# Moving the last two loads of a streaming gradient kernel ahead of a store in the DMA queue

## The chip, the cores and the metric

One core of a Trainium2 chip. The metric is the device time of one execution in microseconds; several executions are timed and the median is given. A profile of one execution has a slightly shorter span than its time (1245.0 us of 1247.06 us in the first profile), so times are compared with times and spans with spans.

## The reference

```python
# x: (8192, 8192) float32
def reference(x):
    return np.gradient(x, axis=1)
```

Inside a row the result is half the difference of the right and the left neighbour; at the two ends it is the plain difference of the last two elements. 268.4 MB are read and 268.4 MB written.

## The kernel before

The rows are cut into 32 sets of 256 rows. A set is 128 partitions with two rows each, 64 KB a partition, 8 MB in all. Three buffers hold three sets. A set is loaded 64 elements to the right of the start of its buffer, and VectorE writes the result over it in place. GpSimd first saves the end differences. Loads and stores all go through one queue, which issues them in program order and waits at each for what it needs: in the profile L30 is issued at 1128.24 us and L31, the next, at 1147.54, S28 having landed at 1147.53.

```python
slots = [pool.tile([P, SH + W], f32, ...) for k in range(NB)]     # NB = 3, SH = 64, W = 2 * 8192

def load(i):                                # waits for the store that frees the buffer
    b = slots[i % NB]
    ins = nc.sync.dma_start(out=b[:, SH : SH + W], in_=x_sets[i])
    loads.append(chain(i, ins, *([stores[i - NB]] if i >= NB else [])))

for i in range(NB):
    load(i)
for i in range(nsets):                      # nsets = 32
    ...                                     # GpSimd: ends of the rows
    last = i == nsets - 1
    nr = 1 if last else R                   # the last set goes in two halves
    for r in range(0, R, nr):
        ins = nc.vector._custom_dve(...)    # half the difference of the neighbours, in place
        ...                                 # VectorE or GpSimd: put the ends in
        ins = nc.sync.dma_start(out=out_sets[i, :, ...], in_=b[:, ...])
        stores[i] = chain(i, ins, placed)
    if i % NB == NB - 1:                    # after each third store: the next three loads
        for k in range(i + 1, min(i + 1 + NB, nsets)):
            load(k)
```

(Cuts are marked with "...".) So the queue holds three loads, three stores, three loads and so on. In what follows L0 to L31 are loads and S0 to S31 stores. The last entries are L27 L28 L29, S27 S28 S29, L30 L31, S30, S31a, S31b. A "turn" is the place where the queue goes over from loads to stores or back.

Of the kernel before, what the change touches and what calls it, by code (L numbers as in the profile page):

```python
# [1 line left out]

# [4 lines left out]


@with_exitstack
def kernel(  # L10
    ctx: ExitStack,
    tc: tile.TileContext,
    x: bass.AP,
    out: bass.AP,
):










    nc = tc.nc
    P = nc.NUM_PARTITIONS  # L27
    n, m = x.shape  # L28
    R = 2  # L29
    NB = 3  # L30
    SH = 64  # L31
    W = R * m
    nsets = n // (P * R)
    f32 = x.dtype

    x_sets = x.rearrange("(s p t) m -> s p (t m)", p=P, t=R)
    out_sets = out.rearrange("(s p t) m -> s p (t m)", p=P, t=R)

    pool = ctx.enter_context(tc.tile_pool(name="pool", bufs=1))
    slots = [pool.tile([P, SH + W], f32, name=f"slot{k}", tag=f"slot{k}") for k in range(NB)]  # L40
    ends = pool.tile([P, nsets, R, 2], f32, name="ends", tag="ends")
    loads, stores = [], [None] * nsets
    in_front = {}

    def chain(i, ins, *needed):



        group, engine = f"slot{i % NB}", ins.ins.engine
        keep = [o.ins for o in needed]  # L50
        if in_front.get(engine, (None,))[0] == group:
            keep.append(in_front[engine][1])
        tc.declare_no_dep(ins.ins, group=group, keep=keep, reason="implied by the needed step")
        tc.add_to_no_dep_group(group, ins.ins)
        in_front[engine] = group, ins.ins
        return ins

    def load(i):
        b = slots[i % NB]
        ins = nc.sync.dma_start(out=b[:, SH : SH + W], in_=x_sets[i])  # L60
        loads.append(chain(i, ins, *([stores[i - NB]] if i >= NB else [])))

    with tc.manual_schedule():
        for i in range(NB):
            load(i)
        for i in range(nsets):
            b = slots[i % NB]
            xin = b[:, SH : SH + W].rearrange("p (t m) -> p t m", m=m)

            ins = nc.gpsimd.tensor_sub(  # L70
                out=ends[:, i, :, :],
                in0=xin[:, :, 1 : m : m - 2],
                in1=xin[:, :, 0 : m - 1 : m - 2],
            )
            at = [chain(i, ins, loads[i])]
            last = i == nsets - 1
            nr = 1 if last else R
            for r in range(0, R, nr):
                c0, c1 = r * m + 1, (r + nr) * m - 1

                ins = nc.vector._custom_dve(  # L81
                    dve_ops.TENSOR_TENSOR_REDUCE_SUB_MAX,
                    out=b[:, c0:c1],
                    in0=b[:, SH + c0 + 1 : SH + c1 + 1],
                    in1=b[:, SH + c0 - 1 : SH + c1 - 1],
                    s0=0.0,
                    s1=0.5,
                )
                halved = chain(i, ins, *at)
                res = b[:, r * m : (r + nr) * m].rearrange("p (t m) -> p t m", m=m)  # L90
                placer = nc.gpsimd if i % 5 in (1, 3) and not last else nc.vector
                ins = placer.tensor_copy(out=res[:, :, 0 : m : m - 1], in_=ends[:, i, r : r + nr, :])  # L92
                placed = chain(i, ins, halved)
                ins = nc.sync.dma_start(
                    out=out_sets[i, :, r * m : (r + nr) * m], in_=b[:, r * m : (r + nr) * m]
                )
                stores[i] = chain(i, ins, placed)
                at = [halved]
            if i % NB == NB - 1:
                for k in range(i + 1, min(i + 1 + NB, nsets)):  # L100
                    load(k)


# [1 line left out]
_INS = ['x']  # L105
_OUTS = [((8192, 8192), 'float32')]


# [23 lines left out]
```

## Time and profile before

| | |
|---|---|
| time, 3 executions | 1247.18 us median (1247.16 to 1247.86) |
| span of the profile | 1245.0 us |
| DMA, share of 16 engines | 99.8% |
| VectorE busy | 45% |
| waits of the queue for stores (before loads) | 373.2 us in total |

Two views matter here. The stretches give, for a stretch of time, its length, the busy time of VectorE and GpSimd, the clock, the DMA share and the GB/s; a DMA packet is counted where it starts. In the order of time each row has a start, a duration, the engine and the operation, and in brackets how long the engine was idle before and what ended that. GpSimd's small subtraction (TENSOR_TENSOR) is the first thing that happens to a set after its load has wholly landed, so its start marks the landing on the slowest of the 16 DMA engines: in the packet records (see the experiments) the engines of the kernel before end L31 from 1202.48 to 1205.05 us, and GpSimd starts on it at 1205.53. These two rows of the kernel before, in the order of time, will be compared with all later runs; they are the landings of L30 and L31:

```profile
1186.19 0.20 POOL L70 TENSOR_TENSOR ends<-slot 128x4 f32<-128x4 f32 x1 [77.05 <-DMA slot<-in_x_dram]
1205.53 0.20 POOL L70 TENSOR_TENSOR ends<-slot 128x4 f32<-128x4 f32 x1 [19.14 <-DMA slot<-in_x_dram]
```

They are 19.34 us apart, eight packets of 2.418 us: the slowest engine lost nothing on L31. The bracket of the second row (19.14 us of idle time) says the same; a larger figure there is lost time.

### The profile page before, as it was taken

The numbers are of one execution on the slowest core, as the hardware profiler recorded it, in microseconds if no ns is written. First come the engines' busy times: TensorE is split into PE (matmuls) and PEld (weight loads), VectorE is DVE, ScalarE is ACT, GpSimd is POOL, SyncE is SP. The second block draws the span as 40 slices with busy tenths as digits, with TensorE's granted clock in tenths as the row PEclk, the third lists the DMA queues.
The fourth block names the chain that finished last, engine by engine and source line by source line (L and its number), as shares of the span: only waits on it lengthen the run. The fifth ranks groups of instructions, "written<-read, shape, count | busy, mean of one in ns | idle before, by whom it ended". The sixth has DMA issues, their size and how long they took to land.

```text
span 1245.0 us, 241 instructions
## 1 busy us (share of the span) xinstructions
DVE 554.8 (45%) x54; POOL 8.8 (1%) x48
## 2 busy tenths in 40 slices
DVE  2850483079009603850582079009603840591083
POOL 0000000000000000000000000000000000000000
DMA  9999999999999999999999999999999999999999
GB/s 404 438 436 419 425 438 438 438 438 438 434 427 421 436 438 438 436 438 432 432 419 438 436 438 432 436 434 432 423 436 436 436 438 436 430 427 430 436 411 404
DMA packets 9361, 536.88 MB, mean 431 GB/s; under 512 B 1040, under 2 KB 1040, under 8 KB 1040
## 3 DMA queue, kind: packets, MB, share of 16 engines
q1 hardware_dynamic: 9360, 536.88, 99.8%
q14 instruction: 1, 0.01, 0.0%
HBM read 268.44 MB, written 268.44 MB: 431 GB/s over the span
## 4 chain that ended last, share of the span: by engine, by line
another core or an unknown queue 74%; DVE 18%; DMA 3%; issue 2%; POOL 1%; SPq 0%; POOLq 0%
DVE slot L81 18%; DMA slot<-in_x_dram 3%; POOL ends L70 0%; POOL slot L92 0%; SPq L60 0%; DVE slot L92 0%; POOLq L127 0%
## 5 line engine op out<-in xcount | busy, mean ns | idle before, releaser
L81 DVE CUSTOM_DVE_ANT_0 slot<-slot 128x16382 f32<-128x16382 f32 (+1 forms) x33 | 551.3, 16706 | 667.9 <-POOL ends L70 667.9
L70 POOL TENSOR_TENSOR ends<-slot 128x4 f32<-128x4 f32 x32 | 6.3, 198 | 988.8 <-DMA slot<-in_x_dram 988.8
L92 DVE COPY slot<-ends 128x4 f32<-128x4 f32 (+1 forms) x21 | 3.6, 172 | 0.7
L92 POOL COPY slot<-ends 128x4 f32<-128x4 f32 x12 | 2.3, 190 | 207.9 <-DVE slot L81 207.9
L116 POOL MEMSET const-bfloat16-1.0<- 128x1 bf16 x1 | 0.1, 102 | 0.0
L116 POOL MEMSET const-uint8-127<- 128x1 uint8 x1 | 0.1, 102 | 0.0
L116 POOL MEMSET const-float32-0.0<- 128x1 f32 x1 | 0.1, 99 | 0.2 <-issue 0.2
L116 POOL MEMSET const-float32-1.0<- 128x1 f32 x1 | 0.1, 99 | 0.0
## 6 DMA issues: line engine op xcount, KB each, us to landing
out_dram<-slot SPq DMA_DIRECT2D x2, 4096.0 KB, 20.2
slot<-in_x_dram SPq DMA_DIRECT2D x32, 58.0
out_dram<-slot SPq DMA_DIRECT2D x31, 40.3
```

The costliest lines, as they stand in the source:

```text
L70: ins = nc.gpsimd.tensor_sub(out=ends[:, i, :, :], in0=xin[:, :, 1 : m : m - 2], in1=xin[:, :, 0 : m - 1 : m - 2],)
L81: ins = nc.vector._custom_dve(dve_ops.TENSOR_TENSOR_REDUCE_SUB_MAX, out=b[:, c0:c1], in0=b[:, SH + c0 + 1 : SH + c1 + 1], in1=b[:, SH + c0 ...
L92: ins = placer.tensor_copy(out=res[:, :, 0 : m : m - 1], in_=ends[:, i, r : r + nr, :])
L116: nc = _bacc.Bacc("TRN2", target_bir_lowering=False, num_devices=1)
```

## The change

The intent is to have the last two loads in early, since the end of the kernel is load, compute, store with nothing left to overlap, and since S29 is ready long ahead of S30 (issued at 1126.63 and 1203.88 us in the profile of before) and can fill the engines later. L30 and L31 are issued after S28 instead of after S29.

```diff
+    n3 = (nsets - 2) // NB * NB
+    assert nsets - 2 == n3
+    next_loads = {i: range(i + 1, i + 1 + NB) for i in range(NB - 1, n3 - NB, NB)}
+    next_loads[n3 - 2] = range(n3, nsets)
 ...
-            if i % NB == NB - 1:
-                for k in range(i + 1, min(i + 1 + NB, nsets)):
+            if i in next_loads:
+                for k in next_loads[i]:
                     load(k)
```

## The prediction

> **What bounds the kernel now.** I read the page first, then the waits of the queue that issues the DMAs, then the order of the last issues in time, and last the DMA share in narrow stretches at the end.
>
> The page shows that nothing but DMA is near its limit:
>
> ```profile
> span 1245.0 us, 241 instructions
> ...
> DVE 554.8 (45%) x54; POOL 8.8 (1%) x48
> ...
> DMA  9999999999999999999999999999999999999999
> GB/s 404 438 436 419 425 438 438 438 438 438 434 427 421 436 438 438 436 438 432 432 419 438 436 438 432 436 434 432 423 436 436 436 438 436 430 427 430 436 411 404
> ...
> q1 hardware_dynamic: 9360, 536.88, 99.8%
> ```
>
> VectorE works 45% of the span; the 16 DMA engines are at 9 tenths in every slice and 99.8% busy on the one queue in use. 536.88 MB is the input read once plus the output written once, so the bytes cannot shrink. The best slices run at 438 GB/s; 536.88 MB at 435 GB/s would be 1234 us, 11 us (0.9%) less than the span. That is more than any reordering can win, and the start and the end have their part in it.
>
> Names: L0 to L31 are the 8 MB loads, S0 to S31 the stores (S31 in two halves, a and b). One 8 MB transfer takes 8.389 MB / 435 GB/s = 19.3 us. The queue's own waits:
>
> ```profile
> SPq L94 <- DVE slot L92: 525.7, 21, 55.9
> SPq L60 <- DMA out_dram<-slot: 373.2, 29, 19.2
> SPq L94 <- POOL slot L92: 298.8, 12, 36.7
> ```
>
> The issuing queue waits nearly always, but for things behind which data is still queued: a load waits for a store two transfers back, while one more is in the engines. Waiting there costs nothing unless the engines run dry. So I looked for a place where they do. The last group in order of time:
>
> ```profile
> 1109.17 17.22 DVE L81 CUSTOM_DVE_ANT_0 slot<-slot 128x16382 f32<-128x16382 f32 x1 [2.13 <-POOL ends L70]
> ...
> 1126.63 0.33 SPq L94 DMA_DIRECT2D out_dram<-slot  x1
> 1128.24 19.64 SPq L60 DMA_DIRECT2D slot<-in_x_dram  x2
> ...
> 1186.42 17.23 DVE L81 CUSTOM_DVE_ANT_0 slot<-slot 128x16382 f32<-128x16382 f32 x1 [59.81 <-POOL ends L70]
> ...
> 1203.88 19.93 SPq L94 DMA_DIRECT2D out_dram<-slot  x3
> ...
> 1205.76 8.69 DVE L81 CUSTOM_DVE_ANT_0 slot<-slot 128x8190 f32<-128x8190 f32 x1 [1.91 <-POOL ends L70]
> ```
>
> S29 is issued at 1126.63, L30 at 1128.24, L31 19.3 us later (1147.54 when that row is looked at alone), then nothing until S30 at 1203.88. S30 can't be issued before VectorE is through with L30's data. L31 is the only transfer between L30's landing and S30, so there the engines can run dry, and narrow stretches show that they do (share and GB/s count a packet where it starts; a packet is 64 KB on one engine and takes 2.4 us, so 16 starts in 0.5 us read 2097 GB/s):
>
> ```profile
> 1166.60:1185.90 19.30, 0.00 (x0) 0.00 (x0) 1.00 1.00 435
> 1185.90:1205.20 19.30, 17.40 (x2) 0.20 (x1) 1.00 0.95 411
> ...
> 1199.80:1200.30 0.50, 0.50 (x1) 0.00 (x0) 1.00 2.72 1180
> 1200.30:1202.20 1.90, 1.90 (x1) 0.00 (x0) 1.00 0.56 241
> 1202.20:1202.70 0.50, 0.50 (x1) 0.00 (x0) 1.00 0.91 393
> 1202.70:1204.70 2.00, 1.11 (x2) 0.00 (x0) 1.00 0.00 0
> 1204.70:1205.20 0.50, 0.00 (x0) 0.00 (x0) 1.00 4.91 2097
> ```
>
> The last packets of L31 start spread over 1199.8 to 1202.7: nine in the first half microsecond (1180 GB/s x 0.5 us / 65.5 KB), seven in the next 1.9 us, then three, on late engines that also started one in the first half microsecond (the 16 engines, three of them twice, are the 19). Nobody starts anything in the next 2.0 us, and all 16 start S30 together at 1204.7 to 1205.2. So there is a hole, 0 to 2.4 us depending on the engine; from the packet records the mean is 1.6 us. But the engines that began last, at 1202.2 to 1202.7, are done 2.4 us later, at 1204.6 to 1205.1: for the slowest engine the hole is about nothing. In the packet records its L31 share ends at 1205.05, and its S30, S31a and S31b shares end 19.32, 9.68 and 9.68 us later, at 1243.73, where the data ends. It never waits.
>
> [...]
>
> **The change part by part.** Removed and added: nothing; 67 instructions on the issuing queue in both, the same on the other engines. The order of instructions shows one move: S28, S29, L30, L31, S30 becomes S28, L30, L31, S29, S30. Each 8 MB transfer is a slot of 19.3 us in the engines; they change places.
>
> 1. L30 waits for S27 as before (1128.2), L31 for S28 as before (1147.5). These issue times don't move. S29, ready at 1126.6, is issued behind L31: about 1147.9, 21 us later.
> 2. While L31 is held, the engines have the rest of S28 (to 1147.3) and L30 (to 1166.6). L31 and S29 are there from 1147.9, 19 us before L30 ends. No hole opens.
> 3. Data slots after: L30 1147.3 to 1166.6, L31 1166.6 to 1185.9, S29 1185.9 to 1205.2, S30 1205.2 to 1224.5, S31 1224.5 to 1243.8. L30 and L31 come 19.3 us earlier, S29 38.6 us later, S30 and S31 stay.
> 4. VectorE on L30: about 1167.1 to 1184.3; S30 issued about 1184.6, some 20 us before its slot. On L31: halves at 1186.4 and 1195.1; S31a issued about 1195.3, S31b 1204.1, 29 and 30 us before their slots. The hole closes: 1.6 us of mean engine idleness goes.
> 5. On the path that sets the end: the slowest engine's own chain of packets. It had about 0.0 us of hole, so it gets back 0.0 us. The leading engines end up to 2.4 us earlier and then have nothing to do. Sum: 1247.18 - 0.0; I take 0.1 us off for S30's start, which then lies behind queued data for every engine. Prediction 1247.1 us.
>
> **The rivals.** (a) The hole is paid back in full. If the 16 engines shared one limit, idle engines would be lost capacity and the end would come 1.6 us earlier: 1245.6 us. Against it: packets take 2.418 us with all 16 busy, and those of the engines that ran alone during the hole take 2.42 to 2.45; no engine goes faster when others are idle. The lag is also each engine's own history: the spread of the finishing times grows from 0.48 us after five transfers to 2.57 us at L31, and nothing lets the late ones catch up. (b) The final compute is exposed. If VectorE's 17.4 us after L31's landing lay bare at the end, moving L31 forward by 19.3 us would win up to that: about 1230 us. Against it: S30's 19.3 us cover the first half (8.7 us, S31a issued at 1214.7 for a slot at 1224.5) and S31a's 9.7 us the second (issued 1223.47, 11 us before its slot). (c) The queue stalls in a new place. If L31's wait for S28 held S29 while the engines ran out, it would cost; with L30's 19.3 us queued ahead and about 1 us from issue to the first packet, there are 18 us of margin. [...] (d) Chance: the lag of the slowest engine comes from scattered slow packets (up to 1 us of excess) and differs from run to run; the three runs spread over 0.7 us.
>
> **Range and chances.** The centre is 1247.1. Below, rival (a) in full gives 1245.6; above, a new small wait or an unlucky set of slow packets gives a microsecond. 1245.5 to 1248.3 should hold it 8 times in 10. Two per cent is 25 us, which no rival but (b) comes near, and that not wholly: faster 0.01, same 0.985, slower 0.005.
>
> **What would show it right or wrong.** Right: L30 and L31 land 39 us after issue in place of 57.9; S29 is issued near 1147.9; the queue's last stores are issued near 1184.6, 1195.3 and 1204.1; the stretch 1185.9 to 1205.2 reads a share of 1.00; VectorE is through by 1204 and not 1223; the data still ends at about 1243.7 and the span stays at 1245. The engines should end spread out by some 2.5 us, not together within 0.2 us. Wrong: all engines end together a microsecond or two earlier (rival a), or a stretch of low DMA share appears between 1147 and 1186 (rival c), or the slow packets bunch in another place.

Its sum came to 1247.18 - 0.0 - 0.1 = 1247.1 us (the 0.1 us is the author's estimate, with no trace behind it).

## The result

| | median | range | executions |
|---|---|---|---|
| before, same job | 1247.59 us | 1247.16 to 1248.12 | 6 |
| changed | 1248.45 us | 1248.12 to 1249.27 | 6 |

The ratio is 1.0008, with a 95% interval of 0.9995 to 1.002: the same, within 2%. Ratios are the mean time of one kernel's fast runs over that of the other's of the same rounds, so not quite the ratio of the medians. The changed kernel is 1.35 us over the predicted 1247.1 us and 0.15 us over the upper end of the range. No gain was forecast and none came; what has to be explained is the microsecond in the other direction.

The page of the changed kernel, where it answers to that of before:

```profile
span 1246.3 us, 241 instructions
...
DVE 554.8 (45%) x54; POOL 8.8 (1%) x48
...
GB/s 404 438 438 433 419 427 438 438 438 438 433 433 429 423 435 438 435 438 431 433 433 433 427 435 431 438 438 435 433 433 438 421 431 438 438 435 433 435 431 358
```

VectorE has done the same work in the same time. The last slice but one moved 431 GB/s where it had moved 411, the last one 358 where it had moved 404: the transfers are packed closer ahead of the end and thin out in it.

The end in order of time (rows between are left out):

```profile
1148.46 57.32 SPq L103 DMA_DIRECT2D out_dram<-slot  x4
1167.45 0.20 POOL L79 TENSOR_TENSOR ends<-slot 128x4 f32<-128x4 f32 x1 [57.76 <-DMA slot<-in_x_dram]
...
1187.50 0.20 POOL L79 TENSOR_TENSOR ends<-slot 128x4 f32<-128x4 f32 x1 [19.85 <-DMA slot<-in_x_dram]
...
1205.25 0.17 DVE L101 COPY slot<-ends 128x2 f32<-128x2 f32 x1
```

S29 is issued at 1148.46, L30 has landed at 1167.45 and VectorE is through at 1205.42, all as forecast. But L31 lands at 1187.50, 20.05 us after L30 and not 19.34: the slowest engine lost 0.71 us there that it did not lose before (0.73 in the packet records, whose step was 20.05 against 19.32).

The stretches of the changed kernel:

```profile
1185.90:1205.20 19.30, 17.43 (x3) 0.20 (x1) 1.00 1.00 435
1202.70:1204.70 2.00, 2.00 (x1) 0.00 (x0) 1.00 0.61 262
...
1239.70:1240.70 1.00, 0.00 (x0) 0.00 (x0) 1.00 1.06 459
1240.70:1243.20 2.50, 0.00 (x0) 0.00 (x0) 1.00 0.34 144
1243.20:1243.90 0.70, 0.00 (x0) 0.00 (x0) 1.00 0.22 94
```

The hole is closed: the share over 1185.9 to 1205.2 is 1.00, and packets go on starting between 1202.7 and 1204.7, where none did before. At the very end the packets are 32 KB. In the first row of the end 14 of them start in 1.0 us (459 GB/s x 1.0 us / 32.8 KB), about the full rate of 435 GB/s; in the next 2.5 us only 11 (full rate would be 33), in the last 0.7 us two. Some engines are done while others still work. In the packet records the first engine ends at 1240.98 and the last at 1245.07, 4.09 us apart; in the kernel before all ended between 1243.57 and 1243.73.

Between these two profiles the data ends 1.34 us later (1245.07 against 1243.73). 0.61 us of it was there before the kernels differ at all: at the end of S28 and of the transfer after it the slowest engine of the changed kernel was already 0.61 us behind that of the other. The rest, 0.73 us, is the step at L31.

### The profile page after: what moved, and what is told of

It is laid out like the page before. It is cut to its first block, busy times and chain, and to the rows that moved or that the text cites. A ratio compares the mean times of both kernels' runs of the same rounds, so it can differ in the third digit from the quotient of the medians.

```text
span 1246.3 us, 241 instructions
## 1 busy us (share of the span) xinstructions
DVE 554.8 (45%) x54; POOL 8.8 (1%) x48
## 4 chain that ended last, share of the span: by engine, by line
another core or an unknown queue 67%; DVE 18%; DMA 10%; issue 2%; POOL 1%; SPq 0%; POOLq 0%
DVE slot L90 18%; DMA slot<-in_x_dram 6%; DMA out_dram<-slot 3%; POOL ends L79 0%; POOL slot L101 0%; DVE slot L101 0%; SPq L62 0%; POOLq L136 0%
```

## The experiments

First, where the late engines get late. "Packet records" are the start, the duration and the size of every DMA packet, kept in the trace; no view prints them. Which engine a packet ran on is inferred: an engine starts its next packet as the last one ends, so the packets fall into 16 chains (in order of time, 99% of the packet starts of the kernel before lie within 0.005 us of the end of the packet 16 places ahead). The "loss" at a transfer is the time from the last engine's end of the transfer before to the last engine's end of this one, less the 19.32 us of an undisturbed transfer.

In the two profiles so far most packets that take over 2.5 us instead of 2.418 us, apart from the very first of the kernel, are the last ones of the last load of a group (89 of 112 in the kernel before, 112 of 114 in the changed one): at L2, L5, L8 and so on, where loads give way to stores. In the profile of before, for instance, all 16 engines had one at the end of L17 (starting 639.0 to 640.4, 2.57 to 3.23 us long), and there was none in the 50 us to either side. The turns from stores to loads show few; they cost the slowest engine at most 0.07 us in these two profiles, though single ones cost up to 0.83 us in later profiles. At the turns from loads to stores the slowest engine lost between 0.0 and 1.4 us, most at the first one. These losses differ from run to run and from engine to engine, which is how the engines drift apart.

That gave theory T: where a store already lies queued while the last load before it is still running, that load's last packets on the late engines are slowed. The kernel before spares itself this at its last turn, since S30 reaches the engines just as L31 ends (its first packets start at 1204.72 to 1205.06 us, and L31 ends on the last engine at 1205.05). The changed kernel, with S29 queued there for 38 us, pays it as at most other turns. (At L17 the leading engines' packets were slow too, before any packet of the store had started, so "late engines" is too narrow. Why the packets are slow stays open.) The rivals: N, all is chance; O, the new places of S29 or of the loads cost something else; H, the hole had been lost time.

**The changed kernel again.** Edit: none.

> The changed kernel once more, five rounds. Theory T (a store that lies queued while the last load before it still runs slows that load's last packet on the engines that are late; the hole of the kernel before spared them this at its last turn from loads to stores): about 0.5 to 0.9 us slower than before, with slow packets (0.3 us or more over 2.42 us) at the end of load 31, which the kernel before has not. Rival N (noise; each run draws its slow packets at random): within 0.3 us of before.

Measured: 1248.77 us against 1247.94 us (ratio 1.0007, 0.9994 to 1.002). In this profile L31 landed 19.48 us after L30 on GpSimd's row; in the packet records the step was 19.60 us, 0.28 us of loss. The sign held, and the loss at L31 was smaller than in the first profile.

**Store 30 ahead of store 29.**

```diff
+                if i == nsets - 3:
+                    held = i, r, nr, placed          # store 29 waits its turn
+                else:
+                    store(i, r, nr, placed)
+                    if i == nsets - 2:
+                        store(*held)                 # after store 30
```

> The changed order, but store 30 goes out ahead of store 29, so that behind load 31 again comes a store that is issued only as load 31 ends; the two loads still lie ahead of store 29. Theory T: the time goes back to that of before, 0.5 to 0.9 us under the changed kernel, and no slow packets at the end of load 31. Rival O (it is the later place of store 29, or the earlier one of the loads, that costs): the time stays at that of the changed kernel. Rival N: all equal within 0.3 us.

Measured: 1248.14 us against 1247.94 us of before (ratio 1.0001, 0.9987 to 1.0015), where the changed kernel had 1248.77. In order of time:

```profile
1168.66 0.20 POOL L85 TENSOR_TENSOR ends<-slot 128x4 f32<-128x4 f32 x1 [57.74 <-DMA slot<-in_x_dram]
1188.01 0.20 POOL L85 TENSOR_TENSOR ends<-slot 128x4 f32<-128x4 f32 x1 [19.14 <-DMA slot<-in_x_dram]
```

The step is 19.35 us: nothing lost at L31. In the packet records the hole is back (a leading engine's next transfer ended about 22.8 us after its L31 and not 19.32), it costs the slowest engine nothing (19.32 us), and there is no slow packet at L31. The loads still lie ahead of S29, so what matters at L31 is when the store behind it comes, not the place of the loads. On the times alone, T and O are not told apart by these five executions; the packets tell them apart.

**The hole closed without moving a load.** Set 30 is computed and stored in halves, in the order of before.

```diff
-            nr = 1 if last else R
+            nr = 1 if i >= nsets - 2 else R
```

> The order of before, but set 30 is computed and stored in halves, so that its first store is issued about 1195 and lies queued 10 us before load 31 ends: the hole is closed without moving any load. Theory T: slower than before by 0.5 to 0.9 us, slow packets at the end of load 31, the engines end apart by 2.5 us or more. Rival O: the same as before. Rival H (the hole was lost time): faster by up to 1.6 us.

Measured: 1248.74 us against 1247.94 us (ratio 1.0005, 0.9993 to 1.0018); the profiled execution was its quickest, 1247.63 us. Its L30 and L31, in order of time:

```profile
1186.41 0.20 POOL L70 TENSOR_TENSOR ends<-slot 128x4 f32<-128x4 f32 x1 [77.07 <-DMA slot<-in_x_dram]
1206.13 0.20 POOL L70 TENSOR_TENSOR ends<-slot 128x4 f32<-128x4 f32 x1 [19.52 <-DMA slot<-in_x_dram]
```

19.72 us and 19.52 us of idle time: a loss of 0.4 us at L31 (0.45 in the packet records, 15 engines with a slow packet), in a kernel whose loads are all where they were. The engines end 2.85 us apart. Closing the hole won nothing, so rival H falls.

**The middle store first, in every group.** If a store that comes just in time spares the turn, every group could have one: of sets 27, 28, 29 the store of 28 is ready about when L29 ends.

```diff
+                if i % NB == 0 and i + 2 < nsets:
+                    held = i, r, nr, placed
+                else:
+                    store(i, r, nr, placed)
+                    if i % NB == 1 and i + 1 < nsets:
+                        store(*held)
```

> The kernel before, but in each of the ten full groups the middle set is stored first and the first set second, so that each turn from loads to stores looks like the last one of before: the store comes just as the group's last load ends. Theory T: the slow packets at the ends of loads 2, 5, 8 ... 29 go or shrink, the lag of the slowest engine stays under 1 us, and the time falls by 2 to 4.5 us against before, to some 1243 to 1246. Rival R (slow packets come [...]not from queued stores): no faster than before; holes of up to 0.3 us a group on the slowest engine make it up to 3 us slower.

Measured: 1254.58 us against 1247.94 us, ratio 1.0053 (1.004 to 1.0065). The forecast of the time was wrong, that of the turns right: at the ends of L2, L5 ... L29 there is no slow packet left, the slowest engine's loss there is 0.02 us or less, and the engines stay within 1.1 us of each other. But the loss came back at the other kind of turn. The stretches around the end of a third store of this kernel:

```profile
348.50:348.80 0.30, 0.00 (x0) 0.00 (x0) 1.00 8.07 3495
348.80:350.90 2.10, 0.00 (x0) 0.00 (x0) 1.00 0.00 0
350.90:351.20 0.30, 0.00 (x0) 0.00 (x0) 1.00 10.62 3495
351.20:353.90 2.70, 0.00 (x0) 0.00 (x0) 1.00 0.00 0
353.90:354.60 0.70, 0.00 (x0) 0.00 (x0) 1.00 3.62 1498
```

3495 GB/s in 0.3 us are 16 packets: all engines start a packet within 0.3 us, 2.4 us later the next one, the store's last; the first packets of the load follow 3.0 to 3.5 us later and not 2.4. The slowest engine lost 1.0 to 1.2 us at nine of the ten turns from stores to loads and 1.5 us at the first, where the kernel before loses 0.0 to 0.5 us in its three profiles, mostly nothing. All of its losses up to L31 sum to 11.58 us in this profile against 4.25, 5.42 and 5.61 us in three of before, which covers the 6.6 us.

**Is it how long the next load has been queued?** In the last kernel each group's first load waited for a store that now goes second, so it was queued 19 us ahead of its turn and not 38 us. Two kernels complete the square: the middle store first with 38 us, and the old order of stores with 19 us. In both, two of the buffers change places from group to group.

```diff
+    def slot_of(i):
+        g, j = divmod(i, NB)
+        return j if j == NB - 1 else (j + g) % 2
 ...
-        b = slots[i % NB]
+        b = slots[slot_of(i)]
```

> As middle_first, but the next group's first load goes into the buffer whose store went out first, so it is issued 38 us ahead of its turn as in the kernel before, not 19 us. Middle_first lost 6.6 us because its slow packets (1 us on all engines) moved to the turns from stores to loads. Theory D (a transfer of the other direction that is queued late makes the turn slow; 38 us ahead is enough): the slow packets go from both turns and the time falls under that of before, to 1243 to 1246. Rival P (the hole starts all engines at the same moment, and a turn taken in step costs all of them about 1 us, wherever it comes): the time stays at about 1254.5.

> The kernel before, but its buffers change places so that each group's first load waits for the second store of the group and is issued 19 us ahead of its turn, not 38 us; the order of stores is that of before. Theory D: slow packets of about 1 us appear at the turns from stores to loads, some 5 to 10 us slower, 1253 to 1258. Rival P: nothing changes, within 0.5 us of before.

Measured: 1254.82 us (ratio 1.0053, 1.0041 to 1.0066) and 1248.28 us (ratio 1.0001, 0.9988 to 1.0013), against 1248.11 us of before. The lead does nothing in either order; theory D falls, and both times are as rival P forecast. What the two slow kernels share is that each group's late store lets the engines start together (0.1 to 0.3 us apart after it in most groups). That they then lose a microsecond at the next turn because they take it in step, as P has it, fits, but no kernel here put them in step in another way, so this stays an argument.

**More turns, and no arithmetic.**

```diff
# alternate: one load after each store from the second on
-            if i % NB == NB - 1:
-                for k in range(i + 1, min(i + 1 + NB, nsets)):
-                    load(k)
+            if 1 <= i < nsets - 2:
+                load(i + 2)
```

> Loads and stores one by one in turn after the first two stores: 30 turns from loads to stores in place of 11, every store queued before the load ahead of it ends. Theory T (each such turn costs the late engines 0.2 to 0.8 us; before, about 4.5 us of lag came from 11 turns): 6 to 10 us slower, some 1254 to 1258. Rival R (slow packets come by themselves with time): within 1 us of before.

Measured: 1249.45 us against 1248.11 us (ratio 1.0009, 0.9995 to 1.0022; four executions). That is far less than the 6 to 10 us that T expected, though over the 1 us of rival R; on four executions it is not clear of the noise. In the order of time, the landings of early and of late loads, two transfers apart:

```profile
159.87 0.20 POOL L70 TENSOR_TENSOR ends<-slot 128x4 f32<-128x4 f32 x1 [21.58 <-DMA slot<-in_x_dram]
199.31 0.20 POOL L70 TENSOR_TENSOR ends<-slot 128x4 f32<-128x4 f32 x1 [39.23 <-DMA slot<-in_x_dram]
239.34 0.20 POOL L70 TENSOR_TENSOR ends<-slot 128x4 f32<-128x4 f32 x1 [39.84 <-DMA slot<-in_x_dram]
...
1131.20 0.20 POOL L70 TENSOR_TENSOR ends<-slot 128x4 f32<-128x4 f32 x1 [20.89 <-DMA slot<-in_x_dram]
1169.89 0.20 POOL L70 TENSOR_TENSOR ends<-slot 128x4 f32<-128x4 f32 x1 [38.50 <-DMA slot<-in_x_dram]
1208.46 0.20 POOL L70 TENSOR_TENSOR ends<-slot 128x4 f32<-128x4 f32 x1 [38.37 <-DMA slot<-in_x_dram]
```

Two transfers take 38.64 us when nothing is lost. The early steps are 39.44 and 40.03 us, the late ones 38.69 and 38.57. In the packet records the engines are 0.7 us apart after five transfers and 5.6 us after forty, and from there on the slowest loses nothing at any turn. So the loss is not a fixed price of a turn. It fits that a loss is paid while the engines turn close together, and that in paying it they drift apart. It is no sharp rule: the changed kernel lost 0.79 us at L31 in one profile with its engines already 3.9 us apart.

The other kernel sends each loaded set straight back, without arithmetic and with a wrong result:

```diff
-            ins = nc.gpsimd.tensor_sub(...)      # and all that follows on VectorE and GpSimd
+            ins = nc.sync.dma_start(out=out_sets[i], in_=b[:, SH : SH + W])
+            stores[i] = chain(i, ins, loads[i])
```

> Loads and stores in the order of before with all arithmetic taken out: the store sends the loaded data back, a wrong result on purpose. Each group's first store is then issued when its load lands, 38 us ahead of its turn. Theory T without VectorE's part: slow packets still stand at the ends of loads 2, 5 ... 29, and at load 31; 1247.5 to 1249. Rival V (VectorE's or GpSimd's use of the memory makes them slow): no slow packets at all, some 1243. Theory D: as rival V, since the lead is 38 us.

Measured: 1248.59 us against 1248.11 us (ratio 1.0002, 0.9987 to 1.0017). The slow packets stand at the ends of L2, L5 ... L29 as ever (losses of 0.07 to 1.13 us of the slowest engine), so neither VectorE nor GpSimd makes them (rival V falls), and stores queued 38 us ahead do not avoid them (D falls again). At L31 the slowest engine lost nothing in this profile.

**One load moved, and looks to size the term.** Only L30 goes ahead of S29.

```diff
-    next_loads[n3 - 2] = range(n3, nsets)
+    next_loads |= {n3 - 2: range(n3, n3 + 1), n3 - 1: range(n3 + 1, nsets)}
```

> The order of before, but only load 30 goes ahead of store 29: store 28, load 30, store 29, load 31, store 30. Both turns from loads to stores at the end (30 to 29, 31 to 30) then have a store that has been queued for 19 us or more, where the changed kernel has one such turn and the kernel before none. Theory T: twice the loss or nearly, 0.8 to 1.8 us slower than before, 1249 to 1250, as long as the engines are not yet so far apart that a turn costs nothing. Rival O (it is store 29's late place or the loads' early one that costs, not the turns): between before and the changed kernel, under 0.6 us slower.

Measured: 1248.92 us against 1248.14 us (ratio 1.0005, 0.9991 to 1.0018), just under T's 0.8 us and above O's 0.6 us; with intervals this wide the time excludes neither. The row of L30's landing shows where:

```profile
1169.16 0.20 POOL L79 TENSOR_TENSOR ends<-slot 128x4 f32<-128x4 f32 x1 [58.65 <-DMA slot<-in_x_dram]
```

58.65 us of idle time, against 57.76 us in the changed kernel: 0.89 us lost at L30, which has become the last load before a store. At L31, the second such turn, the slowest engine lost nothing.

> The changed kernel, one look, to size the term: the slowest engine's step from the end of load 30 to the end of load 31, 19.32 us where nothing is slow. Theory T: 19.5 to 20.2 us in most looks (20.05 and 19.60 so far).

> As after_look_a: 19.5 to 20.2 us by theory T, 19.32 us by rival N.

> The kernel before, one look: the same step at load 31. Theory T: 19.32 us, nothing slow there, as in its first profile, while the ends of loads 2 to 29 again show slow packets.

Measured: the changed kernel 1248.28 and 1247.64 us, with losses at L31 of 0.12 and 0.00 us; the kernel before 1248.14 us, with 0.00 us. Both fell short of T's 19.5 us, and the second was as rival N has it. In this job the changed kernel was no slower than before (1248.14 us, nine executions).

**The size.** So four more runs, in one job on one chip, the edits being those shown above or none.

> The changed kernel, five rounds more. If the turn at load 31 is all: 0.2 to 0.4 us slower than before in the mean, with the step at load 31 at 19.3 to 20.1 us. If something more differs: 0.7 to 1.0 us slower again.

> As after_c: 0.2 to 0.4 us slower in the mean if the turn is all, 0.7 to 1.0 us if not.

> The kernel before under a label of its own, for more of its times and one more profile: 0.0 +- 0.2 us against before, and 19.32 us for the step at load 31.

> The changed order with store 30 ahead of store 29, once more: no slow packets at load 31, its step 19.32 us; within 0.2 us of before if the turn at load 31 is all that the change costs.

Measured: 1248.87, 1248.69, 1248.72 and 1248.99 us, against 1248.58 us (ratios 1.0002, 1.0000, 1.0001 and 1.0001, all with intervals of some 0.13% to either side). Here no difference can be seen in the times: the changed kernel is 0.01 us under before in the mean, where 0.2 to 0.4 us over was forecast. The landings of L30 and L31 in after_d:

```profile
1168.20 0.20 POOL L79 TENSOR_TENSOR ends<-slot 128x4 f32<-128x4 f32 x1 [57.74 <-DMA slot<-in_x_dram]
1188.25 0.20 POOL L79 TENSOR_TENSOR ends<-slot 128x4 f32<-128x4 f32 x1 [19.85 <-DMA slot<-in_x_dram]
```

20.05 us apart again, 0.71 us more than in the kernel before; the packet records say 0.79 (GpSimd's start follows the landing by 0.35 to 0.5 us, so its rows are good to about 0.1 us). All 18 profiles, from the packet records:

| kernel | behind L31 comes | loss of the slowest engine at L31, us | engines with a packet over 2.5 us there |
|---|---|---|---|
| before (3 profiles) | S30, just in time | 0.00, 0.00, 0.00 | 0, 0, 0 |
| store 30 ahead of 29 (2) | S30, just in time | 0.00, 0.00 | 0, 0 |
| 19 us lead (1) | S30, just in time | 0.00 | 0 |
| middle store first (2) | S30, just in time | 0.00, 0.00 | 0, 0 |
| changed (6) | S29, queued 38 us | 0.73, 0.28, 0.12, 0.00, 0.09, 0.79 | 7, 1, 6, 2, 3, 9 |
| set 30 in halves (1) | half of S30, queued 10 us | 0.45 | 15 |
| only L30 moved (1) | S30, queued 20 us | 0.00 (0.89 at L30) | 5 (8 at L30) |
| no arithmetic (1) | S30, queued 19 us | 0.00 | 1 |
| alternate (1) | S30, queued 20 us | 0.00 | 0 |

The mean of the changed kernel's six is 0.34 us. The differences of the mean times of the changed kernel and of before, job by job, were +0.95 (6 and 6 executions), +0.83 (5 and 9), -0.30 (2 and 9) and -0.01 us (10 and 14, with those of before_b). Weighted by nm/(n+m), for n and m executions, they give +0.36 us. That the two figures agree is welcome, but the jobs differ among themselves by more than their own scatter would give, and what differs between jobs stays open (the later ones ran on chips 5, 7, 3 and 6). What is settled is the place and the order of size. The only loss that the change adds on the path to the end stands at L31, and it is a third of a microsecond in the mean. Slow packets there are absent in all eight profiles where the store comes just in time and present in nine of the ten where it is queued. The tenth is alternate, whose engines are 5.6 us apart. A queued store does not always cost the slowest engine time: four of the ten lost nothing, and the kernel before lost at most 0.03 us at L29. The 0.86 us of the first job are more than this; the rest is taken here for luck of the earlier turns, which are the same in both kernels, but that is shown (0.61 us) for the two profiled executions only.

No kernel here beats the one before.

## Why the prediction was right or wrong

- **The bound and the verdict (right).** DMA binds (99.8% of the 16 engines' span, VectorE 45%), and this change of order moved the time by less than 0.1% (ratio 1.0008). Other orders can move more: the middle store first cost 0.5%.
- **Steps 1 to 4 (right).** L30 and L31 landed 38.6 and 39.4 us after issue in place of 57.9, S29 was issued at 1148.46 (1147.9 forecast), the last store about 1205.4 (1204.1), the share of the stretch was 1.00 and VectorE was through at 1205.42 (1204). No hole opened in a new place, so rival (c) was rightly refused.
- **The hole costs the slowest engine nothing (right).** Closing it by halves won nothing, and opening it again cost nothing, against rival (a). Two readings on the way are slightly off and change nothing: the mean hole is 1.5 us and not 1.6, and the packets that ran alone in it took 2.418 us, while those of 2.44 to 2.46 us are the first of S30, started together.
- **Step 5, "so it gets back 0.0 us" (the step that failed).** The sum had a term for what the hole gave back and none for what a queued store costs. The new turn from L31 to S29 took 0.00 to 0.79 us, 0.34 us in the mean, where the prediction took 0.1 us off for S30's start, by estimate. The mis-sized term is -0.1 us; measured, +0.34 us. Its own sign of being wrong, slow packets that bunch in another place, came true at L31.
- **Rival (d), "scattered slow packets" (misread).** Most are not scattered: in the profile of before 89 of 112 stand at the turns from loads to stores. The prediction saw the lag grow from 0.48 to 2.57 us and did not ask at which transfers. Had it, it would have seen a loss of 0.16 to 1.15 us at eight of the eleven such turns, almost none at L5 and none at L29 and at L31, the turn it was about to change.
- **The centre and the range (too low, too narrow).** The centre hung on the median of three executions, 1247.18 us. In the same job six had 1247.59 us, and all 47 executions of the kernel before lie between 1247.16 and 1249.21 us with a mean of 1248.25 us. Of the 1.35 us by which the centre was missed, 0.41 is this level within the job (1247.59 - 1247.18), 0.08 what was taken off (1247.18 - 1247.1), and 0.86 the difference of the two kernels in that job (1248.45 - 1247.59). Of these 0.86 the new turn is 0.34 in the mean; the rest, and that the first three executions were low, counts as luck here: no run shows a cause for it.
- **The engines end apart (right in kind).** About 2.5 us forecast, 4.09 us measured.

## What to carry to other kernels

In this kernel, whose one queue kept the 16 DMA engines 99.8% busy, the end was set by the slowest engine and not by the mean share: a hole of 1.5 us in the mean cost the slowest 0.00 us, and closing it won nothing (set 30 in halves: 1248.74 us against 1247.94). So look at who is last before counting a hole as lost time. Ask of an order of transfers not only whether it leaves holes but what its turns cost: here a turn from loads to stores with the store already queued lost 0.0 to 1.4 us (in the two profiles of the first comparison, packets took up to 3.73 us there in place of 2.418, and the engines' spread grew from 0.48 and 0.58 us after five transfers to 2.57 and 4.09 us at L31), and a change of the last turn was worth a few tenths of a microsecond. The number of turns alone does not tell: 30 in place of 11 cost 1.1 us more in the mean, not clear of the noise, and the kernel with the middle store first in every group cost 6.6 us more with no more turns than before. Take the level of a kernel from more than three executions if tenths of a per cent are to be forecast.
